# Stores queued one step later, squares written over the input, retention states loaded ahead and operand differences made ahead, in a one-core streaming-encoder kernel

## The chip, the cores and the metric

The kernel runs on one core of a Trainium2 chip. The core has five engines that take their own instructions in order: TensorE (PE; its weight loads are shown apart as PEld), VectorE (DVE), ScalarE (ACT), GpSimd (POOL), and SyncE (SP), which here does nothing but issue DMA transfers. The metric is the device time of one execution in microseconds, the median of a few runs.

## The reference

One layer of a hybrid encoder on 2048 prompt tokens, 16 learned meta tokens and 8 running streams of 16 tokens. Batch axes and reshapes are left out here.

```python
h = rms_norm(x, g_pre)
q, k, v, gate, ga, gb = split(h @ w_in)              # 512 wide each
q, k = rope(q), rope(k) * HEAD_DIM ** -0.5
# per chunk of 64 tokens, 4 heads of 128:
scores = einsum('bihd,bjhd->bhij', q, k) * d_intra
out    = einsum('bhij,bjhe->bihe', scores, v) + einsum('bihd,bhde->bihe', q, S) * d_in
S_new  = S * exp(lg * L) + einsum('bjhd,bjhe,hj->bhde', k, v, d_out)
ret    = group_norm(out) * silu(gate)
conv   = silu(layer_norm(causal_depthwise_conv(ga * sigmoid(gb), 31 taps)))
mix    = concat([ret, conv]) @ w_out
x = x + rms_norm(mix, g_post_mix)
h = rms_norm(x, g_pre_mlp)
x = x + rms_norm(relu(h @ w_mlp_in) ** 2 @ w_mlp_out, g_post_mlp)
# out: y of prompt and streams, new states S, new conv caches
```

The streams start from given states (`state_ret`, 8 streams x 4 heads of 128x128), and their new states are outputs.

## The kernel before

**Numbers.** Each fp32 operand of a large matmul is split into two fp32r parts, hi and lo (`split`: ACT copies hi, then DVE or POOL subtracts to get lo), and three matmuls (hi hi, hi lo, lo hi) replace one. PE accumulates in PSUM. Weights are split as they are first read (`fetch`, `split_unit`) and the parts of the mixer's weights are kept in DRAM (`wkeep_in`, `wkeep_out`) and read again from there.

**Mixer.** Tokens lie along the free axis in six groups (`LAY`) of up to 384 columns; group 3 (`SG`) holds the streams, group 5 is `LAST`. For each group the loop runs projections (`glu`, `head_unit`), retention per head (`head_tail`), convolution on DVE (`conv`, `conv_norm`), and then the output projection of the group before (`out_units`), which copies each PSUM tile to `yo` (three buffers) and stores it to `yscr`. Norms need a column sum: `rstd_bcast` (L487) multiplies by a matrix of ones on PE. For the group with the streams `head_tail` reads the given states in tiles `sst` (L1038), multiplies with them (`os`, L1040), adds the update (L1042) and stores to `o_ss` (L1044).

**Between the two halves.** `mlp_in` reads `yscr` back in three passes over 8 row tiles: squares for the norm; the residual sum `x1d`; and `hd`, the normed MLP input. Its tiles come from pool `s` (five buffers).

**MLP.** The first layer's product is made Strassen-like: seven products P1 to P7 of sums of blocks instead of eight, for three pairs of groups (`G` 0, 1, 2). Operand sums for `G` 0 are made by `make_h2` on DVE just as the MLP starts: it loads blocks of `hd` to `st` tiles (three buffers, L616), subtracts (L622) and splits (L384). For `G` 1 and 2 the block differences are made earlier by `differences` (POOL, L661), stored to DRAM (`td`, L662), and `reload` fetches and splits them, lo by turns on POOL and DVE. While pair `G` is multiplied, `prologue(G + 1)` runs `mlp_in` and `differences` for the next pair. The first layer's weight products `wp` are made on POOL for `G` 0 (L322) and read back from `wprod` (L296) for the others; weights sit in nine buffers. `epilogue` norms the result, adds the residual on POOL (L1189) and stores `o_y` (L1191).

**What sets the order.** Side work stands in queues (`norm`, `conv`, `head`, `mlp`) and `tick` advances them by a few steps after each unit of matmuls. The framework then orders the instructions of each engine by priority and its own estimate of readiness, so a line's place in the program is a wish and not an order. After that the order is fixed: each engine, SP too, stands at an instruction until what it waits for is there. All the large transfers are issued by SP.

Of the kernel before, what the change touches and what calls it, by code (L numbers as in the profile page):

```python
# [20 lines left out]
P = 128  # L21
# [148 lines left out]
def build(nc, T):  # L170
    lg = _log_gamma()
    with tile.TileContext(nc, schedule_with_timeline_sim=True) as tc, ExitStack() as top:
# [325 lines left out]
        def add_square(acc, src, k, W, n=D_MODEL, eng=None):  # L498
# [4 lines left out]
            sq = np_.tile([P, WM], F32, tag="s", name="sq", bufs=SB)  # L503
            nc.scalar.activation(out=sq[:, :W], in_=src, func=AF.Square)
# [28 lines left out]
        def s_tile(N):  # L533
            return np_.tile([P, WM], F32, tag="s", name="s", bufs=SB)[:, :N]

        def mlp_in(gi):

# [4 lines left out]

            def loads(src, two):
# [36 lines left out]
            acc = summed()  # L580
            for k, y, xk in loads(lambda k: yscr[gi][k], True):
# [7 lines left out]
            for k, y, _ in loads(lambda k: x1d[G][k][:, off:off + N], False):  # L589
# [6 lines left out]
        OPS = (P1, P2, P6, P5, P7, P3, P4)  # L596
# [3 lines left out]
        td = [None] + [dram.tile([4, 4, P, n], F32, name=f"td{n}") for n in NH2[1:]]  # L600

# [5 lines left out]

        def make_h2(G, which, eng, put):

            n = NH2[G]  # L610
            need = {P1: (0,), P2: (1,), P3: (1,), P5: (0,), P6: (0, 1), P7: (0, 1), P4: (0, 1)}
            for k in range(4):
                bs = {}
                for r in sorted({r for x in which for r in need[x]}):
                    t = st_tile()[:, :2 * n]
                    nc.sync.dma_start(t, hd[G][k + 4 * r])  # L616
                    bs[r, 0], bs[r, 1] = t[:, :n], t[:, n:]
                yield

                def diff(a, b):  # L620
                    t = s_tile(n)
                    eng.tensor_tensor(out=t, in0=a, in1=b, op=ALU.subtract)  # L622
                    return t

                parts = {P1: bs.get((0, 0)), P2: bs.get((1, 0)), P3: bs.get((1, 1))}
                if {P4, P5, P6} & set(which):
                    parts[P5] = diff(bs[0, 1], bs[0, 0])
                if {P4, P6} & set(which):
                    parts[P6] = diff(bs[1, 1], parts[P5])
                for x in which:  # L630
                    if x == P7:
                        parts[x] = diff(bs[1, 1], bs[0, 1])
                    if x == P4:
                        parts[x] = diff(bs[1, 0], parts[P6])
                    yield from put(x, k, parts[x])

        def put_home(G, eng):
            def put(x, k, part):
                t = hops[G, x] if k else home(G, x)
                split(part, t[:, k], t[:, 4 + k], eng)  # L640
                if k == 3:
                    h2_made.add((G, x))
                yield
            return put

        def differences(G):

            n = NH2[G]
            for k in range(4):
                bs = {}  # L650
# [5 lines left out]
                ts = []  # L656
                for i in range(4):
                    x, y = ((bs[0, 1], bs[0, 0]), (bs[1, 1], ts[0] if i == 1 else None), (bs[1, 1], bs[0, 1]),
                            (bs[1, 0], ts[1] if i == 3 else None))[i]
                    t = s_tile(n)  # L660
                    nc.gpsimd.tensor_tensor(out=t, in0=x, in1=y, op=ALU.subtract)  # L661
                    nc.sync.dma_start(td[G][i, k], t)  # L662
                    ts.append(t)
                    yield

# [293 lines left out]
        def head_tail(gi, h, kr, qr, vf):  # L959
# [64 lines left out]
            if smp:  # L1024
                osm = auxp.tile([P, 512], F32, tag="aux", name="os")[:, :P]
                for s0 in range(0, NS, 4):
                    us = auxp.tile([P, 4, P], F32, tag="aux", name="us")
                    for s in (s0, s0 + 2):
# [4 lines left out]
                        for i in range(2):  # L1033
                            nc.tensor.matmul(us[:, s - s0 + i], ks[:, i], vt[:, sblk], start=True, stop=True)
                    for s1 in (0, 2):
                        s = s0 + s1
                        sst = tp.tile([P, 2, P], F32, tag="sst", name="sst", bufs=2)
                        nc.sync.dma_start(sst, T["state"][h][:, s:s + 2, :])  # L1038
                        for i in range(2):
                            nc.tensor.matmul(osm, qdm[:, (s + i) * (P - SL):(s + i) * (P - SL) + P], sst[:, i],  # L1040
                                             start=(s + i == 0), stop=False)
                        nc.vector.scalar_tensor_tensor(out=sst, in0=sst, scalar=float(np.exp(lg[h] * SL)),  # L1042
                                                       in1=us[:, s1:s1 + 2], op0=ALU.mult, op1=ALU.add)
                        nc.sync.dma_start(T["o_ss"][h][:, s:s + 2, :], sst)  # L1044
                nc.tensor.matmul(osm, sd[:, sblk], vt[:, sblk], start=False, stop=True)
# [38 lines left out]
        def out_units(gi, fs=range(8)):  # L1084
            N = LAY[gi]["N"]
            chi, clo = cats[gi]
            for f in fs:
                whi, wlo = next_unit("out", gi, f)
# [4 lines left out]
                nc.scalar.activation(out=yo[:, :N], in_=ps[:, :N], func=AF.Copy)  # L1093
                nc.sync.dma_start(yscr[gi][f], yo[:, :N])
                tick()

        queues["norm"].append(norm_group(0))
        drain("norm")
        for gi in range(len(LAY)):
# [53 lines left out]
        queues["norm"].append(make_h2(0, (P3, P4), nc.vector, put_home(0, nc.vector)))  # L1153

# [15 lines left out]
        def epilogue(G, c, ya, acc, final=False):  # L1170
# [3 lines left out]
            yield WAIT  # L1174
            rb = yield from rstd_wide(acc, n, D_MODEL)
            for k in range(KT):
                y = ytile(ya, c, k, n)
                if last_x1:
# [13 lines left out]
                yield WAIT if slow else 0  # L1192

        NO = KT // FB
# [287 lines left out]
```

## Time and profile before

| | |
|---|---|
| time before, median of 3 runs | 2417.91 us (2410.08, 2417.91, 2423.68) |
| time of the profiled execution | 2409.09 us |
| its span, first to last instruction | 2407.3 us |
| granted TensorE clock, mean over the span | 0.987 of full speed |
| PE / DVE / POOL / ACT busy, share of the span | 96% / 71% / 61% / 42% |

The span is the stretch that the trace covers; the profiled execution's own time is 1.8 us longer. The busy shares are means over stages that are limited by different things. A granted clock of 1.0 is 2.4 GHz, 0.5 is 1.2 GHz.

### The profile page before, as it was taken

To read this page: it belongs to the slowest core of one execution; us is meant where nothing else is said; L and a number is where in the kernel's file an instruction comes from. 1 tells how busy PE (TensorE), PEld (TensorE's weight loads), DVE (VectorE), ACT (ScalarE), POOL (GpSimd) and SP (SyncE) were. 2 spreads that over 40 slices of the span, in tenths; PEclk is the share of its full clock that TensorE was granted. 3 is DMA by queue.
4 is the path that set the end of the run, shared out by engine and by line. 5 is a ranking of instruction groups with operands and counts; after the bars stand their busy time and mean duration, and the time that the engine had idled before them with its cause. 6 is when DMAs were issued, how large, how long until landed. Compare 5 with 4: busy or idle time off the path is not lost. (4 is left out here: it accounts for less than half of the span.)

```text
span 2407.3 us, 41425 instructions
## 1 busy us (share of the span) xinstructions
PE 2312.4 (96%) x14250; PEld 2277.5 (95%) x14250; DVE 1708.5 (71%) x3704; ACT 1005.1 (42%) x2240; POOL 1470.6 (61%) x1532
## 2 busy tenths in 40 slices
PE   8898999998899998999999999999899999999997
PEld 7898999998899998999999999999899999999997
DVE  8999897896997965546543347678776676666666
ACT  5534334123223133544434445344444443444442
POOL 6847232131133113978888776687897747888874
PEclk9999999999999999999999999999999999999998
DMA  8887787897688778858896557676765567565562
GB/s 316 284 313 273 269 291 265 243 329 275 204 275 285 242 251 322 281 203 291 279 321 228 188 203 253 229 237 216 259 215 166 167 222 260 181 203 175 190 216 95
DMA packets 246338, 584.55 MB, mean 243 GB/s; under 512 B 31984, under 2 KB 106480, under 8 KB 246128
## 3 DMA queue, kind: packets, MB, share of 16 engines
q1 hardware_dynamic: 246128, 581.92, 71.2%
q8 instruction: 112, 1.84, 0.3%
q14 instruction: 98, 0.80, 0.1%
HBM read 445.20 MB, written 136.61 MB: 242 GB/s over the span
## 5 line engine op out<-in xcount | busy, mean ns | idle before, releaser
L1227 PE MATMUL mm<-op,wp 128*128 128x384 f32 (+1 forms) x1344 | 441.9, 329 | 13.3 <-DMA wp<-wprod 12.7
L1229 PE MATMUL mm<-op,wp 128*128 128x384 f32 (+1 forms) x1344 | 439.3, 327 | 1.5 <-POOL wp L322 1.5
L1228 PE MATMUL mm<-op,wp 128*128 128x384 f32 (+1 forms) x1344 | 439.8, 327 | 0.0
L835 DVE SCALAR_TENSOR_TENSOR cv<-ext,par,cv 128x384 f32<-128x384 f32 (+1 forms) x720 | 381.8, 571 | 2.0
L514 PE MATMUL mm<-hhi,whi 128*128 128x384 f32 (+2 forms) x992 | 332.6, 336 | 17.4 <-ACT hhi L731 5.4
L516 PE MATMUL mm<-hhi,wlo 128*128 128x384 f32 (+2 forms) x992 | 331.9, 336 | 7.3 <-DMA wlo<-wkeep_in 3.1
L515 PE MATMUL mm<-hlo,whi 128*128 128x384 f32 (+2 forms) x992 | 331.3, 334 | 0.3
L283 POOL TENSOR_TENSOR wlo<-raw,whi 128x512 fp32r<-128x512 f32 x180 | 239.0, 1347 | 127.2 <-ACT whi L282 52.2
L1320 DVE TENSOR_TENSOR ya<-l2y,ya 128x384 f32<-128x384 f32 (+1 forms) x384 | 194.6, 519 | 117.1 <-PE l2y L1317 116.3
L1227 PEld LDWEIGHTS mm<-op,wp 128*128 128x128 f32 x1344 | 252.9, 188 | 21.8 <-DMA wp<-wprod 7.8
L1229 PEld LDWEIGHTS mm<-op,wp 128*128 128x128 f32 x1344 | 252.9, 188 | 1.9 <-POOL wp L322 1.7
L1228 PEld LDWEIGHTS mm<-op,wp 128*128 128x128 f32 x1344 | 253.0, 188 | 0.1
L356 POOL TENSOR_TENSOR wq<-raw,wq 128x256 fp32r<-128x256 f32 x240 | 183.1, 776 | 58.7 <-ACT wq L355 58.0
L514 PEld LDWEIGHTS mm<-hhi,whi 128*128 128x128 f32 x992 | 191.5, 193 | 19.8 <-ACT hhi L731 5.6
L384 POOL TENSOR_TENSOR fo<-c,fo 128x384 fp32r<-128x384 f32 (+1 forms) x168 | 166.2, 990 | 65.3 <-ACT fo L383 64.1
L516 PEld LDWEIGHTS mm<-hhi,wlo 128*128 128x128 f32 x992 | 190.7, 193 | 10.2 <-DMA wlo<-wkeep_in 3.8
L515 PEld LDWEIGHTS mm<-hlo,whi 128*128 128x128 f32 x992 | 191.0, 193 | 1.5 <-DVE hlo L732 1.1
L1320 DVE TENSOR_TENSOR ya<-l2w,ya 128x384 f32<-128x384 f32 (+1 forms) x288 | 143.1, 517 | 19.3 <-PE l2w L1317 16.7
L1241 DVE TENSOR_TENSOR c<-mm,sn 128x384 f32<-128x384 f32 (+1 forms) x144 | 76.5, 532 | 112.7 <-PE mm L1229 74.5
L322 POOL TENSOR_TENSOR wp<-raw,wp 128x512 fp32r<-128x512 f32 x96 | 126.9, 1327 | 43.9 <-ACT wp L321 31.5
L882 POOL TENSOR_TENSOR sw<-sw,sin 128x384 f32<-128x384 f32 (+2 forms) x48 | 48.3, 1006 | 171.0 <-ACT sw L879 168.5
L282 ACT ACTIVATE whi<-raw 128x512 fp32r<-128x512 f32 x192 | 112.9, 623 | 85.4 <-DMA raw<-w_in 19.0
(261 smaller groups left out, 6292.2 us busy)
## 6 DMA issues: line engine op xcount, KB each, us to landing
wp<-wprod SPq DMA_DIRECT2D x224, 512.0 KB, 3.9
raw<-w SPq DMA_DIRECT2D x256, 256.0 KB, 3.8
wprod<-wp SPq DMA_DIRECT2D x112, 512.0 KB, 3.9
whi<-wkeep_in SPq DMA_DIRECT2D x108, 512.0 KB, 6.2
wlo<-wkeep_in SPq DMA_DIRECT2D x108, 512.0 KB, 5.3
raw<-w_in SPq DMA_DIRECT2D x72, 256.0 KB, 5.6
whi<-wkeep_out SPq DMA_DIRECT2D x36, 512.0 KB, 6.0
wlo<-wkeep_out SPq DMA_DIRECT2D x36, 512.0 KB, 5.7
```

What stands on the lines that cost most here:

```text
L283: (nc.vector if i < 24 and i % 4 == 0 else nc.gpsimd).tensor_tensor(out=lo[:, c], in0=raw, in1=hi[:, c].bitcast(F32), op=ALU.subtract)
L322: tt(out=op[:, H:], in0=src, in1=op[:, :H].bitcast(F32), op=ALU.subtract)
L356: nc.gpsimd.tensor_tensor(out=op[:, o + H:o + 2 * H], in0=src, in1=op[:, o:o + H].bitcast(F32), op=ALU.subtract)
L384: (eng or nc.gpsimd).tensor_tensor(out=lo, in0=src, in1=hi.bitcast(F32), op=ALU.subtract)
L514: nc.tensor.matmul(ps, whi(k), ahi(k), start=(k == 0), stop=False)
L515: nc.tensor.matmul(ps, whi(k), alo(k), start=False, stop=False)
L516: nc.tensor.matmul(ps, wlo(k), ahi(k), start=False, stop=(k == nk - 1))
L835: nc.vector.scalar_tensor_tensor(out=o, in0=src(t), scalar=wt, in1=o, op0=ALU.mult, op1=ALU.add)
L1227: nc.tensor.matmul(ps, hi, ops[:, k, :n], start=start, stop=False, skip_group_check=not first)
L1228: nc.tensor.matmul(ps, hi, ops[:, 4 + k, :n], start=False, stop=False, skip_group_check=not first)
L1229: nc.tensor.matmul(ps, lo, ops[:, k, :n], start=False, stop=(k == 3), skip_group_check=not first)
L1320: last_y[0] = nc.vector.tensor_tensor(out=y, in0=ps, in1=y, op=ALU.add)
```

## The change

- `rstd_bcast`: the matmul by ones makes one column instead of 128.
- `add_square` may be given the tile for the square; in `mlp_in`'s second pass it is the tile of the input `xk`, so that one tile fewer of pool `s` is taken per step.
- Stores of `mlp_in`, `differences`, `out_units` and `epilogue` (not the final one) are collected and issued in the next step (`store`).
- `head_tail` asks for the given states at its start, in two tiles of four states from the pool `raw` (five buffers, 256 KB each), instead of tile by tile where they are used (two buffers, 128 KB each). One DVE instruction updates four states instead of two.
- `make_h2` goes. A new `first_differences` makes the four differences for `G` 0 on POOL and stores them to `td[0]`; it is queued while group `LAST`'s heads are computed. `reload` then fetches and splits the seven operands as for the other pairs: 14 loads of 384 KB instead of 24, 14 of the 28 splits' subtractions on POOL instead of none, no difference on DVE instead of 24, and 16 loads and 16 stores of 192 KB and 16 subtractions on POOL ahead of that.

```diff
-                nc.tensor.matmul(ps[:, b, :], acc[:, s:s + P], ones, start=True, stop=True)
+                nc.tensor.matmul(ps[:, b, :1], acc[:, s:s + P], ones[:, :1], start=True, stop=True)
...
+            if sq is None:
+                sq = np_.tile([P, WM], F32, tag="s", name="sq", bufs=SB)
...
+        def store(stores):
+            while stores:
+                nc.sync.dma_start(*stores.popleft())
...
                 for k in range(KT + 1):
+                    store(stores)
                     if k < KT:
                         y = s_tile(N)
                         nc.sync.dma_start(y, src(k))
...
                 nc.gpsimd.tensor_tensor(out=y, in0=y, in1=xk, op=ALU.add)
-                nc.sync.dma_start(x1d[G][k][:, off:off + N], y)
-                add_square(acc, y, k, N)
+                stores.append((x1d[G][k][:, off:off + N], y))
+                add_square(acc, y, k, N, sq=xk)
                 yield
+            store(stores)
...
-                nc.sync.dma_start(hd[G][k][:, off:off + N], y)
+                stores.append((hd[G][k][:, off:off + N], y))
...
+        def first_differences():
+            n = NH2[0]
+            t = xp.tile([P, KT * WM], F32, tag="x", name="df")
+            for k in range(4):
+                b11, b12, b21, b22 = (t[:, (k % 2 * 4 + i) * WM:(k % 2 * 4 + i) * WM + n] for i in range(4))
+                for r, pair in ((0, (b11, b12)), (1, (b21, b22))):
+                    for c in range(2):
+                        nc.sync.dma_start(pair[c], hd[0][k + 4 * r][:, c * n:(c + 1) * n])
+                yield
+                for i, (o, x, y) in enumerate(((b11, b12, b11), (b12, b22, b12), (b22, b22, b11), (b21, b21, b22))):
+                    nc.gpsimd.tensor_tensor(out=o, in0=x, in1=y, op=ALU.subtract)
+                    nc.sync.dma_start(td[0][(0, 2, 1, 3)[i], k], o)
                     yield
...
+            ssts = []
+            for s0 in range(0, NS if smp else 0, 4):
+                ssts.append(rawps[0].tile([P, 512], F32, tag="raw", name="sst", bufs=RB[0]).rearrange(
+                    "p (s d) -> p s d", s=4))
+                nc.sync.dma_start(ssts[-1], T["state"][h][:, s0:s0 + 4, :])
...
-                nc.sync.dma_start(yscr[gi][f], yo[:, :N])
+                store(stores)
+                stores.append((yscr[gi][f], yo[:, :N]))
                 tick()
+            store(stores)
...
+                queues["mlp"].append(first_differences())
...
-        queues["norm"].append(make_h2(0, (P1, P2, P7), nc.vector, put_home(0, nc.vector)))
+        queues["norm"] += [reload(0, x) for x in (P1, P2, P7)]
         out_units(LAST - 1, range(SPLIT, 8))
-        queues["norm"].append(make_h2(0, (P6, P5), nc.vector, put_home(0, nc.vector)))
+        queues["norm"] += [reload(0, x) for x in (P6, P5)]
...
-                for lo, w, col in segments(G, c):
-                    nc.sync.dma_start(T["o_y"][k * P:(k + 1) * P, col:col + w], y[:, lo:lo + w])
+                stores.extend((T["o_y"][k * P:(k + 1) * P, col:col + w], y[:, lo:lo + w]) for lo, w, col in segments(G, c))
+                if final:
+                    store(stores)
```

**Place 1, SP, the states.** SP's rows between the stores of one head's first two tiles and the load of the next two, before:

```order
L1044 DMA o_ss<-sst 128x256 x2
L257 DMA wlo<-wkeep_in 128x1024
L549 DMA s<-yscr_100 128x384
L1094 DMA yscr_101<-yo 128x384
L256 DMA whi<-wkeep_in 128x1024
L1038 DMA sst<-state 128x256 x2
```

and now, where five of the eight loads stand, among the output projection of group 1 (`yscr_100`), two groups ahead of their use:

```order
L959 DMA sst<-state 128x512
L539 DMA yscr_100<-yo 128x384
L375 DMA wkeep_out<-whi 128x1024
L256 DMA whi<-wkeep_out 128x1024
L539 DMA yscr_100<-yo 128x384
L959 DMA sst<-state 128x512
L377 DMA wkeep_out<-wlo 128x1024
L959 DMA sst<-state 128x512
```

The loads were behind the stores that free their tiles; now five are far ahead of the heads, and only the last three follow a store.

**Place 2, SP and POOL, the start of the MLP.** SP's rows where the last group's output projection begins (`yscr_104`), before:

```order
L1094 DMA yscr_103<-yo 128x384
L616 DMA st<-hd_108 128x768 x7
L304 DMA raw<-w 128x512 x2
L257 DMA wlo<-wkeep_out 128x1024
L256 DMA whi<-wkeep_out 128x1024
L1094 DMA yscr_104<-yo 128x384 x3
```

and now (L666 is `reload`, `td_111` is `td[0]`):

```order
L539 DMA yscr_103<-yo 128x384
L666 DMA st<-td_111 128x2x384
L666 DMA st<-hd_108 128x2x384 x2
L304 DMA raw<-w 128x512 x3
L257 DMA wlo<-wkeep_out 128x1024
L539 DMA yscr_104<-yo 128x384 x2
```

Three loads of operand tiles stand ahead of the weights there instead of seven. On POOL the splits of the operands (`op`) now stand among the last heads' gating (`rn`), the splits of the concatenated input (`clo`) and the first weight products (`wp`); before, the rows were

```order
L1078 TENSOR_TENSOR rn<-rn,gs 128x384
L384 TENSOR_TENSOR clo<-rn,chi 128x384
L1078 TENSOR_TENSOR rn<-rn,gs 128x384
L384 TENSOR_TENSOR clo<-rn,chi 128x384
L384 TENSOR_TENSOR clo<-z_10044,chi 128x384
```

and now they are

```order
L384 TENSOR_TENSOR op_10972<-st,op_10972 128x384
L384 TENSOR_TENSOR op_11017<-st,op_11017 128x384 x2
L1070 TENSOR_TENSOR rn<-rn,gs 128x384
L384 TENSOR_TENSOR clo<-rn,chi 128x384
L384 TENSOR_TENSOR op_11094<-st,op_11094 128x384 x2
L1070 TENSOR_TENSOR rn<-rn,gs 128x384
L384 TENSOR_TENSOR op_11139<-st,op_11139 128x384
L384 TENSOR_TENSOR clo<-rn,chi 128x384
```

Of the 14 splits on POOL eight stand ahead of the last `rn`, two more ahead of the first `wp`, four among the `wp`.

**Place 3, SP, the residual's stores.** SP's rows in the second pass of `mlp_in` for a group of `G` 2, before:

```order
L549 DMA s<-yscr_104 128x384
L554 DMA s<-x 128x384
L585 DMA x1d_107<-s 128x384
L549 DMA s<-yscr_104 128x384
L296 DMA wp<-wprod 128x1024
L554 DMA s<-x 128x384
L585 DMA x1d_107<-s 128x384
L549 DMA s<-yscr_104 128x384
```

and now (L539 is `store`):

```order
L555 DMA s<-yscr_104 128x384
L560 DMA s<-x 128x384
L555 DMA s<-yscr_104 128x384
L539 DMA x1d_107<-s 128x384
L296 DMA wp<-wprod 128x1024
L560 DMA s<-x 128x384
L555 DMA s<-yscr_104 128x384
L539 DMA x1d_107<-s 128x384
```

The store has moved behind the next load of `s`; against the weights `wp` it stands where it stood. The stores of `o_y` in the epilogue of `G` 0 have not moved against their neighbours at all.

## Rows read from the trace of the kernel before

**Rows 1.** The page: span, and busy time of each engine.
```profile
span 2407.3 us, 41425 instructions
PE 2312.4 (96%) x14250; PEld 2277.5 (95%) x14250; DVE 1708.5 (71%) x3704; ACT 1005.1 (42%) x2240; POOL 1470.6 (61%) x1532
```

**Rows 2.** PE's waits: engine, line, releaser: us in total, times, longest.
```profile
PE mm L1227 <- DMA wp<-wprod: 12.7, 18, 1.5
PE os L1040 <- DMA sst<-state: 5.9, 2, 4.4
...
PE mm L516 <- DMA wlo<-wkeep_out: 3.6, 1, 3.6
...
PE mm L514 <- ACT chi L383: 3.0, 2, 2.8
...
PE mm L1229 <- POOL wp L322: 1.5, 1, 1.5
...
PE mm L514 <- ACT yo L1093: 0.7, 2, 0.5
```

**Rows 3.** Busy us of each engine by stretch, then granted clock, DMA share, GB/s.
```profile
602.00:612.00 10.00, 4.26 (x33) 3.62 (x31) 9.67 (x23) 4.93 (x10) 3.01 (x4) 1.00 0.71 239
612.00:619.00 7.00, 6.31 (x24) 6.31 (x25) 4.61 (x12) 1.48 (x4) 3.27 (x4) 0.52 0.26 88
...
926.00:933.00 7.00, 5.87 (x17) 4.86 (x17) 6.96 (x13) 3.60 (x7) 3.46 (x4) 0.51 0.67 216
...
946.00:950.00 4.00, 3.28 (x11) 3.28 (x12) 0.00 (x0) 0.49 (x1) 0.00 (x0) 0.57 1.04 411
...
2391.00:2407.30 16.30, 0.00 (x0) 0.00 (x0) 10.42 (x19) 0.00 (x0) 7.39 (x9) 0.58 0.41 131
```

**Rows 4.** The same view, two longer stretches.
```profile
905.00:985.00 80.00, 69.94 (x376) 65.81 (x374) 48.76 (x84) 34.56 (x71) 39.92 (x30) 0.94 0.90 322
1590.00:1765.00 175.00, 162.08 (x898) 155.87 (x897) 142.04 (x261) 77.67 (x188) 149.95 (x184) 0.99 0.74 242
```

**Rows 5.** SP's timeline from 604 to 614: start, us, what it issues.
```profile
606.78 0.91 SPq L1044 DMA_DIRECT2D o_ss<-sst  x2
610.52 0.81 SPq L1038 DMA_DIRECT2D sst<-state  x2
```

**Rows 6.** SP's timeline from 918 to 985.
```profile
922.79 14.95 SPq L616 DMA_DIRECT2D st<-hd  x7
937.84 0.85 SPq L304 DMA_DIRECT2D raw<-w  x2
938.74 0.42 SPq L257 DMA_DIRECT2D wlo<-wkeep_out  x1
...
941.33 1.00 SPq L257 DMA_DIRECT2D wlo<-wkeep_out  x1
```

**Rows 7.** SP's waits from 900 to 1000.
```profile
SPq L616 <- DVE s L622: 15.7, 10, 2.8
```

**Rows 8.** POOL's groups by shape: busy us, mean ns, idle before.
```profile
L384 POOL TENSOR_TENSOR op<-st,op 128x384 fp32r<-128x384 f32 x14 | 15.7, 1131 | 3.7 <-ACT op L383 2.7 <-DMA raw<-w 0.9
...
L661 POOL TENSOR_TENSOR s<-st 128x384 f32<-128x384 f32 x8 | 8.1, 1012 | 3.3 <-DVE ya L1333 2.9 <-DMA hd<-s 0.4
```

**Rows 9.** DVE's instructions that read tile s: duration ns min/median/max, first and last start.
```profile
L384 DVE TENSOR_TENSOR op<-s,op x16: 540/556/1660, 901.4 to 985.2; 128x384 fp32r<-128x384 f32 x16
L622 DVE TENSOR_TENSOR s<-st x12: 548/556/1679, 899.1 to 978.9; 128x384 f32<-128x384 f32 x12
```

**Rows 10.** POOL's timeline from 930 to 985; idle before in brackets.
```profile
957.57 1.31 POOL L322 TENSOR_TENSOR wp<-raw,wp 128x512 fp32r<-128x512 f32 x1 [12.29 <-DMA raw<-w]
```

**Rows 11.** SP's waits from 1590 to 1765.
```profile
SPq L585 <- POOL s L584: 21.2, 11, 4.9
```

**Rows 12.** PE's timeline around one matmul by ones (three blocks, two passes each).
```profile
906.99 0.83 PE L487 MATMUL st<-cst,cacc 128*128 128x128 f32 x6
907.66 0.49 PE L1072 MATMUL ot<-cst,on 128*128 128x128 f32 x3
```

**Rows 13.** The weight loads of these matmuls: duration ns min/median/max.
```profile
L487 PEld LDWEIGHTS st<-cst,acc x60: 187/192/333, 13.4 to 734.1; 128*128 128x128 f32 x60
L487 PEld LDWEIGHTS st<-cst,cacc x34: 187/192/334, 173.4 to 907.4; 128*128 128x128 f32 x34
```

**Rows 14.** DMA issues: KB each, median us to landing.
```profile
st<-hd SPq DMA_DIRECT2D x38, 384.0 KB, 5.2
...
yscr<-yo SPq DMA_DIRECT2D x40, 192.0 KB, 6.5
```

More of the change, by code (lines that the diff above doesn't have):

```diff
@@ L496, in rstd_bcast, with add_square @@
             return rb[:, :W]
-        def add_square(acc, src, k, W, n=D_MODEL, eng=None):
+        def add_square(acc, src, k, W, n=D_MODEL, eng=None, sq=None):
             if k == 0:
@@ L502, in add_square @@
                 return
-            sq = np_.tile([P, WM], F32, tag="s", name="sq", bufs=SB)
+            if sq is None:
+                sq = np_.tile([P, WM], F32, tag="s", name="sq", bufs=SB)
             nc.scalar.activation(out=sq[:, :W], in_=src, func=AF.Square)
@@ L541, in mlp_in, with loads @@
             early = G == 0
-            def loads(src, two):
+            def loads(src, two, stores=()):
                 ahead = []
                 for k in range(KT + 1):
+                    store(stores)
                     if k < KT:
@@ L580, in mlp_in @@
             acc = summed()
-            for k, y, xk in loads(lambda k: yscr[gi][k], True):
+            stores = deque()
+            for k, y, xk in loads(lambda k: yscr[gi][k], True, stores):
                 nc.vector.scalar_tensor_tensor(out=y, in0=y, scalar=pcol("g_post_mix", k), in1=rs, op0=ALU.mult,
@@ L584, in mlp_in @@
                 nc.gpsimd.tensor_tensor(out=y, in0=y, in1=xk, op=ALU.add)
-                nc.sync.dma_start(x1d[G][k][:, off:off + N], y)
-                add_square(acc, y, k, N)
+                stores.append((x1d[G][k][:, off:off + N], y))
+                add_square(acc, y, k, N, sq=xk)
                 yield
+            store(stores)
             rs = yield from norm(acc)
-            for k, y, _ in loads(lambda k: x1d[G][k][:, off:off + N], False):
+            for k, y, _ in loads(lambda k: x1d[G][k][:, off:off + N], False, stores):
                 nc.vector.scalar_tensor_tensor(out=y, in0=y, scalar=pcol("g_pre_mlp", k), in1=rs, op0=ALU.mult,
                                                op1=ALU.mult)
-                nc.sync.dma_start(hd[G][k][:, off:off + N], y)
+                stores.append((hd[G][k][:, off:off + N], y))
                 yield
-        OPS = (P1, P2, P6, P5, P7, P3, P4)
+            store(stores)
         HOME = {P1: "hhi", P2: "hlo", P6: "chi", P5: "clo", P7: "x", P3: "hhi", P4: "hlo"}
         hops, h2_made = {}, set()
-        td = [None] + [dram.tile([4, 4, P, n], F32, name=f"td{n}") for n in NH2[1:]]
+        td = [dram.tile([4, 4, P, n], F32, name=f"td{G}") for G, n in enumerate(NH2)]
         def home(G, x):
@@ L606, in home @@
             return hops[G, x]
[L608 to L644, printed above, removed]
         def differences(G):
             n = NH2[G]
+            stores = deque()
             for k in range(4):
@@ L1034, in head_tail @@
                             nc.tensor.matmul(us[:, s - s0 + i], ks[:, i], vt[:, sblk], start=True, stop=True)
[L1035 to L1044, printed above, removed]
+                    sst = ssts[s0 // 4]
+                    for i in range(4):
+                        nc.tensor.matmul(osm, qdm[:, (s0 + i) * (P - SL):(s0 + i) * (P - SL) + P], sst[:, i],
+                                         start=(s0 + i == 0), stop=False)
+                    nc.vector.scalar_tensor_tensor(out=sst, in0=sst, scalar=float(np.exp(lg[h] * SL)), in1=us,
+                                                   op0=ALU.mult, op1=ALU.add)
+                    nc.sync.dma_start(T["o_ss"][h][:, s0:s0 + 4, :], sst)
                 nc.tensor.matmul(osm, sd[:, sblk], vt[:, sblk], start=False, stop=True)
@@ L1086, in out_units @@
             chi, clo = cats[gi]
+            stores = deque()
             for f in fs:
@@ L1093, in out_units @@
                 nc.scalar.activation(out=yo[:, :N], in_=ps[:, :N], func=AF.Copy)
-                nc.sync.dma_start(yscr[gi][f], yo[:, :N])
+                store(stores)
+                stores.append((yscr[gi][f], yo[:, :N]))
                 tick()
+            store(stores)
         queues["norm"].append(norm_group(0))
@@ L1147, in build @@
         rate["norm"] = 4
-        queues["norm"].append(make_h2(0, (P1, P2, P7), nc.vector, put_home(0, nc.vector)))
+        queues["norm"] += [reload(0, x) for x in (P1, P2, P7)]
         out_units(LAST - 1, range(SPLIT, 8))
-        queues["norm"].append(make_h2(0, (P6, P5), nc.vector, put_home(0, nc.vector)))
+        queues["norm"] += [reload(0, x) for x in (P6, P5)]
         mlp_on.append(1)
         out_units(LAST)
-        queues["norm"].append(make_h2(0, (P3, P4), nc.vector, put_home(0, nc.vector)))
+        queues["norm"] += [reload(0, x) for x in (P3, P4)]
         def prologue(G):
@@ L1175, in epilogue @@
             rb = yield from rstd_wide(acc, n, D_MODEL)
+            stores = deque()
             for k in range(KT):
+                if not final:
+                    store(stores)
                 y = ytile(ya, c, k, n)
@@ L1189, in epilogue @@
                 eng.tensor_tensor(out=y, in0=y, in1=xk, op=ALU.add)
-                for lo, w, col in segments(G, c):
-                    nc.sync.dma_start(T["o_y"][k * P:(k + 1) * P, col:col + w], y[:, lo:lo + w])
+                stores.extend((T["o_y"][k * P:(k + 1) * P, col:col + w], y[:, lo:lo + w]) for lo, w, col in segments(G, c))
+                if final:
+                    store(stores)
                 yield WAIT if slow else 0
+            store(stores)
         NO = KT // FB
```

3 lines of the change are left out of this document (2 added, 1 removed).

## The prediction

> **What bounds the kernel now.** I read the page first: PE is busy 2312.4 of 2407.3 us [rows 1], so 95 us is all that any edit off PE can give back, and 16.3 us of it is the tail after the last matmul, which this change leaves alone [rows 3]. PE's matmuls run 2312.4/14250 = 0.162 us apart on average, so PE's order is a clock for the rest: an output-projection unit of 24 matmuls is 3.9 us.
>
> Next, PE's own waits, which say who was late [rows 2]. Five of the six are for the parts that the diff touches: the states `sst` (5.9 us), weights `wlo` held in SP's queue (3.6), the last group's operand `chi` (3.0), the first `wp` (1.5), and `wp` read back from `wprod` (12.7 in 18 small pieces).
>
> Third, the stretches around these waits, for the clock. Right after the state stall PE is busy 6.31 us at a granted clock of 0.52, so almost all at 1.2 GHz, after a stretch of 10 us in which it worked 4.26. The same is seen at 926 (0.51) and 946 (0.57) [rows 3]. A stall thus costs its own length and then about half of the slow stretch: 0.48 x 6.31 = 3.0 us after the state stall, 0.49 x 5.87 = 2.9 at 926, 0.43 x 3.28 = 1.4 at 946.
>
> Last, SP's timeline, because four of these waits are transfers that were issued late. All of it is against the profiled execution's 2409.09 us. That lies 8.8 us below the median of 2417.91; the middle of the four known times (2409.09, 2410.08, 2417.91, 2423.68) is 2414.0, and the sum is put against that at the end.
>
> **Part 1, the states.** Before, SP issues the load of a head's next two tiles only when the stores of the two before have landed: store at 606.78, load at 610.52 [rows 5]; PE's longest wait for it is 4.4 us, 5.9 in all [rows 2]. Now five of the eight loads stand two groups ahead (place 1), and the last three follow stores of earlier heads, which by then are long past. The raw buffers they take are free there, since all weights of that stage come from `wkeep`. Worth 5.9 + 3.0 = 8.9 us at most; 0 if the next wait (DVE is busy 9.67 of 10 us there [rows 3]) simply takes over. PE stands still for a transfer in that place and not for DVE, so I am near the upper end, and take 7.
>
> **Part 2, the differences.** From 922.79 SP spends 14.95 us on seven loads of `hd` tiles that wait for DVE to free one of three buffers; the weights behind them leave at 938.74 and 941.33 [rows 6], and SP's wait for DVE L622 sums to 15.7 us [rows 7]. PE waits 3.6 us for the weights, plus 1.4 of slow clock after it. Now three loads stand there instead of seven (place 2). The 24 differences (0.556 us each [rows 9], 13 us) and 14 of 28 splits leave DVE, where they stood between the steps of the last `conv_norm`; this can bring `chi` forward, whose wait is 3.0, with 2.9 of slow clock behind it. Upper bound 3.6 + 1.4 + 3.0 + 2.9 = 10.9.
>
> Against it POOL gets 14 splits of 1.131 us and 16 differences of 1.012 [rows 8], 32 us. The cover: POOL stands idle 12.29 us for `raw` loads that the same SP hold delays [rows 10], and is busy 39.92 of 80 us there [rows 4]. Four splits, 4.5 us, fall among the first `wp`, where PE already waited 1.5; without the cover they all show, so the lower bound is -4.5. I take +5: the hold shrinks by four of seven loads but not to nothing. The 16 differences, their 16 loads and 16 stores fall under the last group's projections. SP may stand at a store until POOL is done, at most 4.9 us at once in the nearest rows [rows 11]; nine weight buffers are more than three units, some 12 us of cover. Taken as 0; -5 if the cover is gone.
>
> **Part 3, stores a step later.** From 1590 to 1765 SP stands 21.2 us, at most 4.9 at once, at `x1d` stores waiting for POOL [rows 11], and PE is busy 162.08 of 175 [rows 4]: 12.9 us idle, the upper bound. But place 3 shows that the store moved past a load of `s` and not past `wp`, for which PE waits, and `o_y` did not move. POOL is busy 149.95 of 175 us, close to a bound of its own. I take 2, from 0 to 12.9. For `yscr` the store now leaves 3.9 us later; landing takes 6.5 [rows 14], 10.4 together, and `yo` has three buffers, 11.7 us. That covers it by 1.3 us, and three PSUM tiles behind `yo` add more; PE's wait for `yo` is 0.7 in all [rows 2]. If SP is held, ACT stands at `yo`, and behind it the splits of `whi` and `chi`. Taken 0, to -5. Squares over the input free one of three tiles a step, so loads of `s` go out sooner, into DMA queues that are 0.74 busy [rows 4]: 0.
>
> **Part 4, one column.** The matmul by ones is 94 passes [rows 13]; six take 907.66 - 906.99 = 0.67 us [rows 12], 0.11 each, 10.5 us in all: the upper bound. The 128-column weight load in front of each stays. No row shows a matmul of one column, so 0 is the lower bound; I take 2, since the weight load stays and many of these lie where PE waits anyway. The Trainium skill (TensorE: Matmul & The Clock Gate, LDWEIGHTS) has the weight load last its column count over 1.2, 107 ns for 128 columns whatever the rows; by that, an estimate, the load alone fills the 0.11 us and this part gives 0, the sum being 2 us less. The rows give 187 to 192 ns for one load, overlapped with others, so they do not decide it.
>
> **Sum:** 7 + 5 + 2 + 2 = 16 us, 2409.1 - 16 = 2393.1 on the profiled execution, and 2414.0 - 16 = 2398 for the median.
>
> **Rivals.** (a) All covers hold: 8.9 + 10.9 + 12.9 + 10.5 = 43 less, 2371 for the median. For it: each piece is a measured wait. Against: POOL at 86% and DVE at 81% in the third. (b) The edits do not do what they say: the framework orders by its own estimate of readiness, so stores stay where they stood and the stalls shift to the next late engine. Only part of the states' gain stays, some 5 us: 2409. For it: the unmoved `o_y` and `wp`; DVE's 9.67 of 10. The whole order of the early groups also shifts by a few instructions, worth some us either way. (c) Slower: POOL is made to wait. Eight splits stand ahead of the last `rn` (place 2). Each needs its `st` load (landing 5.2 us [rows 14]) and ACT's half; if SP is held as it was, 14.95 us, POOL stands with `rn`, `clo`, and so `chi` behind it. Price: 14.95 + 8 x 1.131 = 24 us, with 4.3 of slow clock 28, less the 11 of the other parts: 17 slower, 2431. It decides from where the last `rn` is more than 11 us late. Against: POOL has idle time ahead of these `rn`, and the first four loads stand well ahead.
>
> The Trainium skill (SBUF — State Buffer, Who interferes with whom) adds to (c) that a GpSimd instruction and a DVE one with two SBUF inputs exclude each other for a whole instruction. The rows agree: L622 and L384 take 0.556 at the median and up to 1.68 [rows 9]. As a mechanism here: 30 POOL instructions of 1.01 to 1.13 us, at most 32 us of DVE held; DVE is free 31 of 80 us from 905 [rows 4], so it is hidden unless it falls in `conv_norm`'s chain. There eight of them make 9 us, and the time 2407: inside (b).
>
> **How the numbers follow.** Half a per cent, 12 us, is about what a measurement of this kernel can tell from no change. Forecast (10 to 30 us gained, 2384 to 2404): 0.50. (a): 0.08. (b): 0.30. (c): 0.12, of which 0.10 is over half a per cent. Faster than 2405.8: 0.58; within: 0.32; slower: 0.10. The range leaves out the lower end of (a) and most of (c): 2374 to 2419.
>
> **What would show it.** Part 1: no wait of `os` for `sst`, and a clock of 1.0 after it. Part 2: no SP hold near 15 us ahead of the last projection, and `wp` on POOL without a 12 us idle before. Part 3: SP's wait at `x1d` little changed. Part 4: L487's spacing under 0.11 us. It is wrong if PE's waits for `chi`, `clo` or `wp` grow, if ACT stands at `yo`, or if PE's idle total, now 95 us, stays.

## The result

| | median, us | runs | ratio to the kernel before |
|---|---|---|---|
| before | 2415.16 (2410.08 to 2423.68) | 11 | |
| after | 2400.24 (2387.72 to 2410.43) | 11 | 0.9928 [0.9914, 0.9943] |
| after, taken again beside its parts | 2396.91 (2392.34 to 2400.83) | 6 | 0.9905 [0.9891, 0.992], against 2419.9 (23 runs) |

The change gains 0.6% to 1.0%, 15 to 23 us of some 2418: the medians lie 14.9 us apart in the first measurement (the ratio on record there, 0.9928, stands for 17) and 23.0 in the second. The forecast was 2398; both medians after lie inside its range, 2374 to 2419.

**Which execution a trace shows.** The traced execution of the kernel after is the slowest of its eleven, and that of the kernel before, at 2409.09, was faster than any of its eleven, so the two spans, 2408.6 and 2407.3 [rows 1], show no gain. Experiments 1 and 5 give a second trace of each: spans of 2394.9 and 2416.8. Below, e5 is this second trace of the kernel before.

The page of the kernel after, its first lines, against [rows 1]:

```profile
span 2408.6 us, 41400 instructions
...
PE 2313.7 (96%) x14250; PEld 2276.9 (95%) x14250; DVE 1685.0 (70%) x3658; ACT 1001.1 (42%) x2240; POOL 1499.5 (62%) x1562
```

DVE lost 23.5 us of work and POOL gained 28.9: the differences and splits that were moved.

PE's waits in the kernel after, whole span, as in [rows 2] (line numbers have moved):

```profile
PE mm L1228 <- DMA wp<-wprod: 12.6, 17, 1.8
PE l2y L1316 <- DVE ya L1321: 7.6, 6, 2.4
...
PE mm L1228 <- DVE c L1242: 5.3, 3, 3.3
...
PE mm L517 <- DMA wlo<-wkeep_out: 1.3, 1, 1.3
...
PE mm L515 <- ACT chi L383: 0.9, 1, 0.9
```

The wait for `sst` (5.9) is gone, as are those for the first `wp` (1.5) and `yo` (0.7, absent from e5 too). `wlo` fell from 3.6 to 1.3, `chi` from 3.0 to 0.9. The wait for `wp` out of `wprod` did not move: 12.7 and 12.6. Two waits for DVE have grown: that of PE in the MLP's second layer (`l2y`) for the sums `ya`, from 2.2 to 7.6 (that of its other product, `l2w`, for the same sums fell from 2.5 to 0.8), and that of the first layer for DVE's `c`, from 0.2 to 5.3.

Windows of e5, then of the kernel after: length, busy us of PE, PEld, DVE, ACT and POOL, granted clock, DMA share, GB/s. The last two of each answer to [rows 4].

```profile
500.00:660.00 160.00, 143.26 (x883) 140.38 (x882) 132.47 (x348) 44.93 (x101) 39.76 (x43) 0.95 0.79 267
905.00:985.00 80.00, 72.61 (x393) 68.67 (x391) 50.23 (x89) 35.70 (x74) 38.99 (x29) 0.94 0.92 332
1590.00:1765.00 175.00, 161.40 (x900) 154.54 (x899) 146.34 (x263) 79.46 (x195) 148.71 (x181) 1.00 0.73 239
```
```profile
500.00:660.00 160.00, 155.70 (x1008) 153.12 (x1008) 145.78 (x385) 51.24 (x117) 47.84 (x51) 0.98 0.81 282
905.00:985.00 80.00, 72.61 (x402) 69.71 (x401) 26.82 (x31) 37.64 (x80) 58.06 (x50) 0.98 0.79 290
1590.00:1765.00 175.00, 158.79 (x858) 152.44 (x857) 134.91 (x248) 74.29 (x183) 140.59 (x174) 0.96 0.70 230
```

The gain is in the first window: PE works 12.4 us more of the 160 at 0.98 in place of 0.95, and gets 1008 matmuls done in place of 883. In the second it does 402 in place of 393; in the third it does fewer, 858 for 900. These windows are equal in time and not in work, since the kernel after is some 14 us ahead when the second begins.

To sum such differences over the program I set the start of the n-th of the 14,250 matmuls in each trace against the n-th of e5 (us, negative is earlier; ahead of matmul 3600 the kernels differ by under 7). The framework gives each kernel an order of its own, so the n-th is not always the same matmul: of those ahead of marks 3600 and 3900 up to 18 are others, worth about 1 us by the spacing of their widths; from 5400 on the marks stand behind the same work but for 2 matmuls.

| matmul (time in e5) | 3600 (577) | 3900 (643) | 5400 (878) | 6300 (1045) | 9300 (1579) | 11100 (1914) | last (2400) |
|---|---|---|---|---|---|---|---|
| before | -2.2 | -2.3 | -3.1 | -1.0 | -5.8 | -8.1 | -9.5 |
| after | +4.2 | -13.9 | -14.4 | -18.7 | -18.0 | -7.1 | -8.3 |
| 1 after again | -1.4 | -21.6 | -22.6 | -27.6 | -28.5 | -22.0 | -22.0 |
| 2 states | -4.0 | -21.4 | -25.8 | -23.5 | -21.0 | -18.6 | -17.6 |
| 3 differences | -0.1 | -4.4 | -3.8 | -8.0 | -6.3 | -5.2 | -6.0 |
| 4 stores, squares | -2.2 | -4.0 | -8.6 | -8.0 | -9.4 | +0.1 | -0.6 |
| 6 states, late loads | +1.6 | -16.4 | -19.1 | -17.6 | -16.1 | -14.0 | -14.3 |
| 7 without stores, squares | -4.1 | -23.8 | -19.8 | -22.1 | -20.1 | -18.5 | -19.4 |
| 8 column | -2.1 | 0.0 | -3.0 | -2.5 | -0.9 | +1.9 | +0.9 |
| 9 squares | +1.6 | 0.0 | -3.9 | -2.7 | -3.7 | -0.1 | -1.1 |
| 10 deferred stores | -1.3 | -3.2 | -1.0 | +0.1 | -0.4 | +1.2 | -0.5 |
| 11 two states, five buffers | -1.7 | -19.0 | -20.8 | -21.2 | -22.0 | -21.2 | -21.4 |
| 12 states, differences | -1.2 | -17.2 | -18.6 | -22.2 | -21.2 | -21.3 | -22.1 |

Two traces of one kernel differ by up to 15 us by such a count (after and 1 at 1914), so only steps that several kernels share are read from it: 16 to 20 us gained between 577 and 643 with more buffers for the states, against 4.3 at most without; 2.3 to 5 gained between 878 and 1045 with the differences', against 0.4 at most without; 6.5 to 11 lost between 1579 and 1914 with stores and squares together, against 2.8 at most in those with neither.

### The profile page after: what moved, and what is told of

The parts are those of the page before. It is cut to its first block, busy times and chain, and to the rows that moved or that the text cites. A ratio compares the mean times of both kernels' runs of the same rounds, so it can differ in the third digit from the quotient of the medians.

```text
span 2408.6 us, 41400 instructions
## 1 busy us (share of the span) xinstructions
PE 2313.7 (96%) x14250; PEld 2276.9 (95%) x14250; DVE 1685.0 (70%) x3658; ACT 1001.1 (42%) x2240; POOL 1499.5 (62%) x1562
## 4 chain that ended last, share of the span: by engine, by line
PE 71%; DMA 11%; DVE 10%; POOL 3%; issue 3%; ACT 1%; SPq 1%; DVEq 0%; POOLq 0%; ACTq 0%
PE mm L1228 7%; PE mm L1229 7%; PE mm L1230 7%; PE mm L517 6%; PE mm L516 6%; PE mm L515 6%; DMA wp<-wprod 3%; DVE cv L824 2%; PE l2y L1316 2%; PE l2y L1318 2%; PE l2y L1317 2%; PE mma L515 2%; DMA s<-yscr 2%; PE mma L516 2%; PE mma L517 2%
## 5 line engine op out<-in xcount | busy, mean ns | idle before, releaser
L1228 PE MATMUL mm<-op,wp 128*128 128x384 f32 (+1 forms) x1344 | 444.2, 331 | 19.6 <-DMA wp<-wprod 12.6
L1242 DVE TENSOR_TENSOR c<-mm,sn 128x384 f32<-128x384 f32 (+1 forms) x144 | 76.6, 532 | 130.9 <-PE mm L1230 83.7
```

The costliest lines, as they stand in the source:

```text
L1228: nc.tensor.matmul(ps, hi, ops[:, k, :n], start=start, stop=False, skip_group_check=not first)
```

## The experiments

Theory: the states' buffers carry the gain, the differences add a little, stores and column nothing. Rival: the gain comes from stores or from a general shift of the order. Each ratio is to runs of the kernel before in the same session.

**1, 5: each kernel again.**

> The changed kernel once more, for a second profile, because its first profiled execution (2410.43 us) was the slowest of its eleven and so shows 15 us less of the gain than the medians. Counting matmuls, that trace is 5 us behind the one of before at matmul 3600, 12 ahead at 3900, 18 ahead at 6000 to 7200, and gives 19 back between 7200 and 11100. Theory: the gain of 18 us around the states and 6 at the start of the MLP belongs to the kernel and comes again within 3 us; the loss after 7200 is mostly of that execution, and comes back at 0 to 10. Rival: the loss is the kernel's own, and comes back at 15 to 20. Both: ratio 0.991 to 0.995.

> The kernel before once more, for a second profile: the first profiled execution (2409.09 us) is the fastest of all executions of it so far. Theory: the 8 to 16 us that every other trace gives back to it between matmul 7200 and 11100 is that one execution's luck; this one is 6 to 12 us behind it there, and equal within 3 us up to matmul 3600 and from 3600 to 3900. Rival: it repeats the first within 3 us everywhere, and the loss after 7200 belongs to the edits.

Measured: 0.9905 [0.9891, 0.992] and 2418.58 us. The first trace of the kernel before was a short one.

**2: the states' edit alone** on the kernel before; the loads stand at the head's start, as in the change.

```diff
-                        sst = tp.tile([P, 2, P], F32, tag="sst", name="sst", bufs=2)
-                        nc.sync.dma_start(sst, T["state"][h][:, s:s + 2, :])
+                    sst = ssts[s0 // 4]
```

> The kernel before with the states' edit alone. Theory: the states carry most of the change; PE's wait for sst goes from 5.9 us to under 0.5, the lead at matmul 3900 is 10 to 18 us, and it stays: ratio 0.993 to 0.996. Rival: the lead comes only together with the other edits (free buffers and an earlier order of the stage's side work), or the next late engine takes it back: lead under 6 us, ratio 0.998 to 1.001.

Measured: 2398.99, ratio 0.9913 [0.9899, 0.9927]; 21 us, as much as the whole change. The forecast had 7 for it.

**6: four states a tile from the five buffers, but the load at its use.**

```diff
-                        sst = tp.tile([P, 2, P], F32, tag="sst", name="sst", bufs=2)
+                    sst = rawps[0].tile([P, 512], F32, tag="raw", name="sst", bufs=RB[0]).rearrange(
+                        "p (s d) -> p s d", s=4)
+                    nc.sync.dma_start(sst, T["state"][h][:, s0:s0 + 4, :])
```

> The states' edit alone with the load written where it was, at the use, and only the buffers changed (four states to a tile, five buffers from the raw pool). Theory: the buffers carry it, since the framework lifts a load as soon as its tile is free wherever it is written: ratio 0.990 to 0.993, lead of 18 to 21 us at matmul 3900. Rival: asking at the head's start carries it: ratio over 0.996, lead under 8 us.

Measured: 2397.44, 0.992 [0.9898, 0.9942]. SP issues the loads in the same order as in 2: the place in the program adds nothing.

**11: two states a tile as before, one line changed.**

```diff
-                        sst = tp.tile([P, 2, P], F32, tag="sst", name="sst", bufs=2)
+                        sst = rawps[0].tile([P, 512], F32, tag="raw", name="sst", bufs=RB[0])[:, :256].rearrange(
+                            "p (s d) -> p s d", s=2)
```

> The kernel before with one line changed: the tile of two states comes from the five-buffer raw pool in place of a pool of two. Loads are still written at their use, two states each. If the number of buffers carries the gain of the states' edit: 15 to 21 us gained between 574 and 643 us, ratio 0.990 to 0.994. If the size of the tile does (four states, half as many vector operations of 679 in place of 414 ns): under 5 us, ratio 0.998 to 1.000.

Measured: 2397.19, 0.9906 [0.9888, 0.9924]. Number of buffers, not size of tile or place of the load. The view of tile `sst` in e5 (counts, durations in ns, what the users of the tile waited for, who waited for them), then in 11:

```profile
L1038 SPq DMA_DIRECT2D sst<-state x16: 328/341/670, 16.4 to 641.0; - x16
...
  DMA sst<-state: 11.5, 4
...
  POOL qdm L999: 11.4, 2
  PEld os L1040: 6.0, 2
  PE os L1040: 5.5, 2
```
```profile
L1039 SPq DMA_DIRECT2D sst<-state x16: 332/422/637, 327.2 to 605.9; - x16
...
  PE ob L1051: 1.3, 1
  POOL qdm L999: 1.1, 1
```

With two buffers the last load leaves at 641.0, since each waits for the store of the pair before it; with five, at 605.9. PE's own wait for it is only 5.5 us. POOL, which makes the next head's `qdm` (the queries that `os` multiplies with the states) in a single buffer, stood 11.4 us until `os` had read the last one; with five buffers 1.1. But DVE stood too, at the update of `sst`. Its waits from 500 to 660, in the first trace of the kernel before, then in e5 (where the profile puts the same wait down to a weight load):

```profile
DVE sst L1042 <- PE os L1040: 10.8, 3, 8.2
```
```profile
DVE sst L1042 <- DMA whi<-wkeep_in: 8.9, 1, 8.9
```

In e5 a pair of states is stored at 569.73, the next is asked for at 575.94 and lands at 580.38, `os` runs at 581.57, and DVE, idle since 573.28, goes on at 582.21. DVE's idle time in front of `sst` sums to 8.7 to 12.6 us in each of the seven traces with two buffers, and to 0.0 in each of the seven with five. POOL's wait at `qdm` does not part them so: it is 5.7 and 5.8 in the two traces of the whole change, which has the gain.

The one line also changes the order of PE's matmuls, at 293 places between 570 and 700 us. A shift of the order alone is not the gain: 4 and 9 change 101 and 157 places there, keep DVE's idle time (12.6 and 12.0) and gain no more than 2 us between 577 and 643. What share the new order has beside the freed DVE was not run apart.

**3: the differences' edit alone** (`first_differences` and `reload` for `make_h2`).

```diff
-        queues["norm"].append(make_h2(0, (P1, P2, P7), nc.vector, put_home(0, nc.vector)))
+        queues["norm"] += [reload(0, x) for x in (P1, P2, P7)]
```

> The kernel before with the differences' edit alone (make_h2 replaced by first_differences and reload). Theory: worth 4 to 8 us at the start of the MLP, PE's waits for wlo and chi there nearly gone: ratio 0.996 to 0.999. Rival: POOL's 30 instructions more (32 us) show among the weight products and the last heads: ratio 1.000 to 1.004.

Measured: 2412.7, 0.9969 [0.9957, 0.9981], 7.5 us by the ratio.

**4, 9, 10: stores and squares; squares alone; stores of `mlp_in` and `differences` alone.**

```diff
-                add_square(acc, y, k, N)
+                add_square(acc, y, k, N, sq=xk)
...
-                nc.sync.dma_start(x1d[G][k][:, off:off + N], y)
+                stores.append((x1d[G][k][:, off:off + N], y))
```

> The kernel before with the deferred stores and the squares over the input alone (yscr, x1d, hd, td, o_y; no states, no differences, 128 columns). Theory: the framework's order puts the stores back where they were against the weights, so nothing: ratio 0.998 to 1.002. First rival: loads of s in front of stores free SP: 0.994 to 0.998. Second rival: this edit makes the loss seen between 1590 and 1800: ratio 1.003 to 1.007 and the loss seen there in its trace.

> The kernel before with the squares' new place alone (the square of x1 goes over the input tile, no s buffer for it); every store stays where it was. Stores and squares together gained about 5 us at 640 to 740 us and gave back 7 to 11 us between 1579 and 1914 us. If the squares make the late loss (the input tile is held until its square has been added, so the next loads come later): matmul 9300 to 11100 loses 6 to 10 us against the kernel before, and the ratio is 1.001 to 1.004. If the deferral of the stores makes it: that stretch loses under 3 us, and the ratio is 0.998 to 1.001.

> The kernel before with the stores of x1, of the norm's result and of the differences queued a step later, the squares in a buffer of their own as before. If the deferral makes the late loss (tiles of the s ring are held a step longer and the vector engine runs in bunches): 6 to 10 us lost between matmul 9300 and 11100, ratio 1.001 to 1.004, and the wait of TensorE for ya's work on the vector engine grows from 2.4 us to 6 or more. If the squares make it: under 3 us lost there, the gain at 640 to 740 us stays, ratio 0.996 to 0.999.

Measured: 1.0017 [1.0001, 1.0033], 1.0013 [0.9998, 1.0027], 1.0005 [0.9992, 1.0019]: nothing, or a loss of up to 0.3%. In the table 4 loses 9.5 us between 1579 and 1914, 9 loses 3.6 and 10 loses 1.6. The two do not add up to the 9.5, and they decide little, since kernels with neither edit lose up to 2.8 there; the deferral of `yscr` and of `o_y`, in 4 alone, was not run apart. PE's waits for `ya` from 1560 to 1900 in e5, in 10, in 9 and in 4:

```profile
PE l2w L1315 <- DVE ya L1320: 4.0, 4, 1.9
PE l2y L1315 <- DVE ya L1320: 2.4, 2, 2.2
```
```profile
PE l2y L1327 <- DVE ya L1332: 2.4, 2, 2.2
PE l2w L1327 <- DVE ya L1332: 2.3, 2, 2.0
```
```profile
PE l2y L1316 <- DVE ya L1321: 6.1, 7, 2.4
PE l2w L1316 <- DVE ya L1321: 1.2, 2, 1.0
```
```profile
PE l2y L1336 <- DVE ya L1341: 8.3, 8, 2.5
...
PE l2w L1336 <- DVE ya L1341: 0.7, 2, 0.5
```

The wait of `l2y` grows with the squares, but that of `l2w` for the same sums shrinks. Together they are 6.4 in e5, 4.7 in 10, 7.3 in 9 and 9.0 in 4; the kernels with neither edit have 4.7 to 7.7. So the squares alone move the wait more than they add to it, and only both edits together go beyond. I suspected that DVE then runs the norm's steps in longer bunches; their run lengths do not bear it out (one run of five in 9 as in e5). What makes the loss stays open.

**7: the change without stores and squares.**

```diff
-                add_square(acc, y, k, N, sq=xk)
+                add_square(acc, y, k, N)
```

> The changed kernel without the deferred stores and the squares over the input (states, differences and the one column stay). Theory: those two edits cost some 4 us here as they did alone, so this is the better kernel: ratio 0.986 to 0.990 to the kernel before. Rival: the cost shown alone was a matter of the order in that build, and here nothing changes: ratio 0.990 to 0.993, as the changed kernel.

Measured: 2400.68, 0.9931 [0.9912, 0.995], no better than the change. Stores and squares may gain ahead of 1579 what they lose behind it: in the table, 1 stands at -28.5 there and ends at -22.0, 12 (which has neither) at -21.2 and -22.1. The first trace of the change, at -18.0 there, does not show such a gain, so this stays open.

**8: one column alone.**

```diff
-                nc.tensor.matmul(ps[:, b, :], acc[:, s:s + P], ones, start=True, stop=True)
+                nc.tensor.matmul(ps[:, b, :1], acc[:, s:s + P], ones[:, :1], start=True, stop=True)
```

> The kernel before with the one-column matmul alone. Theory: six passes take as long as before, because the weight load of 128 columns in front of each sets the pace: 0.10 to 0.11 us a pass, ratio 0.999 to 1.001. Rival: a pass is shortened to about half, 0.05 us: 94 passes give 4 to 5 us, ratio 0.997 to 0.9985.

Measured: 0.9995 [0.9979, 1.0012]. PE's timeline of 8, beside [rows 12]:

```profile
907.06 0.72 PE L487 MATMUL st<-cst,cacc 128*128 128x1 f32 x6
907.65 0.53 PE L1072 MATMUL ot<-cst,on 128*128 128x128 f32 x3
```

Six passes take 0.59 us to the next matmul instead of 0.67. Inside the group the starts lie 112 ns apart in both kernels: 128 times fewer columns and the same pace. Only the last pass of a group is shorter, by 0.08 us; with some 16 groups of six that is 1.3 us, too little to measure.

**12: states and differences alone**, the best candidate that the parts suggested.

```diff
-                nc.tensor.matmul(ps[:, b, :1], acc[:, s:s + P], ones[:, :1], start=True, stop=True)
+                nc.tensor.matmul(ps[:, b, :], acc[:, s:s + P], ones, start=True, stop=True)
```

(and stores and squares as before the change)

> The change without its deferred stores, squares and one column: states and differences alone. If the parts add up as measured apart (states 0.9913, differences 0.9969): ratio 0.988 to 0.990, some 2391 us, better than the change in full. If the differences' 7 us are hidden once the states have moved the MLP's start, or if the stores' early gain is needed: ratio 0.991 to 0.994, no better than the change.

Measured: 2396.68, 0.9899 [0.9882, 0.9917], beside 0.9905 for the change and 0.9906 for the one line of 11. None of the three can be told from the others. States and differences together give 24.4 us (20 to 29), the sum of 2 and 3 is 28.5, so how far the two add is not settled. Two builds can also lie 0.3% apart without a cause that was found: 12 differs from 7 by the column alone, which gave nothing in 8, and yet 7 lies at 0.9931 and 12 at 0.9899 (their intervals just overlap).

## Why the prediction was right, and where its terms were not

The total was right: 16 us forecast, 15 to 23 measured, and the sign has its cause in the first two parts, as predicted. But the sum hit through terms that missed: states 7 for 21, differences 5 for 7.5, stores 2 for -4 alone (about 0 in the whole), column 2 for 1. Measured apart the parts make some 26 to 30, more than the whole, so that the total came out is in part luck.

**Part 1, the states: mechanism right, size a third.** The step that failed is the upper bound, "5.9 + 3.0 = 8.9 us at most": it took PE's wait for `sst` and its slow clock for all that the two buffers cost. Behind it stood the reading that PE "stands still for a transfer in that place and not for DVE"; in the first trace too PE waits there for DVE's `gs` (the gate, 3.3), `cacc` (the convolution norm's sum of squares, 2.0) and `kr` (the rotated keys, 1.9), which [rows 2] leaves out. The chain of the two buffers (store, landing, load, landing, `os`) also held DVE, for 8.9 us at once, and what PE then waited for carried DVE's names. In e5 from 500 to 660:

```profile
PE os L1040 <- DMA sst<-state: 5.5, 2, 4.0
PE mm L514 <- DVE gs L953: 4.0, 1, 4.0
PE st L487 <- DVE cacc L509: 2.0, 1, 2.0
PE ot L1072 <- ACT on L1067: 1.9, 1, 1.9
PE mm L933 <- DVE kr L881: 1.9, 1, 1.9
```

In 11, where the buffers alone changed:

```profile
PE ot L1073 <- ACT on L1068: 2.0, 1, 2.0
PE ob L1051 <- DVE sst L1043: 1.3, 1, 1.3
PE rb L495 <- DVE dg L491: 1.1, 1, 1.1
```

The waits for `on` (the normed heads, which ACT writes from DVE's statistics: 1.9, at 587.65) and `cacc` (2.0, at 590.33) follow straight on DVE's stand: the statistics of that head and the convolution's norm are DVE's next work after 582.21. That the wait for `gs` at 597.65 does too, by way of loads that SP issued only after the states' load at 587.01, is argued from the order of the rows and not shown; `kr`, at 543.88, comes ahead of this stand. In 11 the waits for `gs`, `cacc` and `kr` have gone with `sst`, though DVE's work in them is the same. So the busy DVE (9.67 of 10 us [rows 3]), on which rival (b) built, was catching up and was not the limit. The clock behind the place is whole, as the prediction said (0.52 before, [rows 3]). In the kernel after it is 0.83 from 602 to 612, then:

```profile
612.00:619.00 7.00, 7.00 (x46) 7.00 (x44) 7.00 (x19) 1.76 (x5) 0.00 (x0) 1.00 0.66 216
```

From the windows: 12.4 us of PE's time, and (0.05 x 143) - (0.02 x 156) = 4.0 us of clock, 16.4 together, near the 18 to 20 of the table for the two traces of the change. PE's idle total, 94.9 us in the first traces before and after, is 102.8 in e5 and 87.8 in 1.

**Part 2, the differences: right in place and nearly in size.** SP's 14.95 us hold is gone, and `chi`, `wlo` and the first `wp` came nearer as said. The cover for the 16 differences held: they ran from 744 to 775, and between the marks at 643 and 878 the table shows no loss above 0.6 for the change or for 3. It is thin, though: 7 loses 4.0 there. A new wait took back some 3 us, which the prediction had named but thought hidden: DVE held by POOL. DVE's timeline of the kernel after, then POOL's (start, us; idle before in brackets):

```profile
946.62 9.02 DVE L384 TENSOR_TENSOR op<-st,op 128x384 fp32r<-128x384 f32 x3 [26.20 <-PE mm L1230]
955.56 0.54 DVE L1242 TENSOR_TENSOR c<-mm,sn 128x384 f32<-128x384 f32 x1
```
```profile
945.04 2.58 POOL L322 TENSOR_TENSOR wp<-raw,wp 128x512 fp32r<-128x512 f32 x2
947.57 1.32 POOL L312 TENSOR_TENSOR s<-raw 128x512 f32<-128x512 f32 x1
948.82 1.04 POOL L384 TENSOR_TENSOR op<-st,op 128x384 fp32r<-128x384 f32 x1
949.79 1.33 POOL L322 TENSOR_TENSOR wp<-raw,wp 128x512 fp32r<-128x512 f32 x1
951.04 2.02 POOL L384 TENSOR_TENSOR op<-st,op 128x384 fp32r<-128x384 f32 x2
952.99 1.29 POOL L313 TENSOR_TENSOR raw<-raw 128x512 f32<-128x512 f32 x1
```

Three splits, 0.556 us each at the median before [rows 9], take 9.02; the first lasts 8.08, to 954.70, and POOL's unbroken row of instructions ends at 954.28. Behind it stands `c` (L1242), for which PE waits 3.3 us. All kernels here with this edit show such a split at that place, of 5.9 to 8.8 us; 2 and the kernel before have none. The Trainium skill (SBUF — State Buffer, Who interferes with whom) has a DVE instruction with two SBUF inputs contend with a GpSimd one that reads SBUF, for a pair of ports that is locked exclusively. The trace agrees and goes further: the wait lasted through seven POOL instructions.

**Part 3, stores: right that little comes; what SP shows is the squares' doing.** I said that SP's wait at `x1d` would stay, and took the squares for 0. SP's waits from 1590 to 1765, e5 then after:

```profile
SPq L296 <- PE mm L1229: 22.4, 11, 4.2
SPq L585 <- POOL s L584: 21.4, 11, 4.9
SPq L296 <- PE l2w L1316: 9.7, 3, 4.1
```
```profile
SPq L296 <- PE l2y L1318: 22.0, 12, 4.5
SPq L296 <- PE mm L1230: 21.8, 10, 4.1
...
SPq L539 <- POOL s L592: 4.3, 4, 3.6
```

The wait for POOL at the `x1d` store fell from 21.4 to 4.3 (the deferred store is L539). The same wait with the stores alone deferred (10), then with the squares alone (9):

```profile
SPq L538 <- POOL s L591: 19.5, 10, 4.3
```
```profile
SPq L586 <- POOL s L585: 6.6, 5, 3.6
```

So the deferral left it about where it was, as predicted, and the squares took it away, which the prediction had not seen. It won nothing: in the rows shown of the kernel after SP stands longer at `wp` instead (L296), 43.8 us for 32.1, until PE frees a weight buffer. SP's hold lay in the shadow of that; PE's waits for `wp` stay at 7.8 us against 6.7 from 1560 to 1900. The upper bound of 12.9, PE's whole idle time there, was not this edit's to win.

**Part 4, the column: 0 to 1 instead of 2.** The lower bound was right. The Trainium skill (TensorE: Matmul & The Clock Gate, LDWEIGHTS) gives, by its formula, 107 ns for the weight load of 128 columns; the 112 ns between the passes agree, and by it the term would have been 0.

**Rivals.** (a) fell: the first cover paid above its bound, the second 7.5 of 10.9, the other two nothing. (b) fell on its own ground, the DVE: the states' gain stayed whole in 2 and 11. (c) did not come: SP's longest hold at `reload`'s `st` is 3.4 us, `clo` costs 1.3 in all, but its mechanism in small (POOL keeps others waiting) is PE's 3.3 us at `c`.

## What to carry to other kernels

The price of a double buffer whose reload waits for a store is not the wait that names it. Follow the chain of loads from the first to the last, see which engine stands at its end and what else that engine, working in order, has yet to do (here DVE, 8.9 us at once), and take all of PE's idle and slow time in the stretch as upper bound (here 16.7 us idle and some 7 of slow clock for a gain of 16 to 20). The hold on SP's queue was worth nothing here, since its next instructions waited for PE's weight buffers anyway. Of five edits here, one line (five buffers for two) gave the same as all.

## What the runs showed of the hardware

How long POOL can hold a DVE instruction with two SBUF inputs: 8.08 us for a split whose median was 0.556 [rows 9], and 5.93 in the second trace of the kernel after. In both it ended 0.42 us after the last of POOL's unbroken row. Only one split at this place was held so, and PE lost 1.2 to 4.0 us by it in the five traces with the edit. So work that fills POOL's gaps, as 14 splits and the weight products do here, can give back in one piece, some 7.5 us, part of what it takes off DVE. It is not the edit's alone: between 1405 and 1435, at the reload for a later pair, eleven of the fourteen traces show one split held for 7.20 to 7.23 us in the same way, e5 among them.
